# A second layer's modulation vectors: six products with ones and transposes, or 96 multiply-and-sums along the free axis

## The chip, the cores and the metric

The kernel runs on one core of one Trainium2 chip. The metric is the device time of one execution in microseconds. Engines are named as in the profile: PE (TensorE, with PEld for its weight loads), DVE (VectorE), ACT (ScalarE), POOL (GpSimd) and SP (SyncE, which issues nearly all DMAs here).

## The reference, cut to what matters

Two sequences, a prompt of 256 and a sample of 512 tokens of width 1024, go through a trunk of two layers. Layer 0 mixes with a bidirectional mLSTM, layer 1 with sliding-window attention; each then has a convolutional feed-forward block. In every layer six vectors of 1024 numbers, made from a condition vector, shift, scale and gate what flows through. All is float32.

```python
def trunk(x, c, adaln_w, adaln_b, norm_g, ...):
    for l in range(DEPTH):
        mod = jax.nn.silu(c) @ adaln_w[l] + adaln_b[l]
        sh1, sc1, g1, sh2, sc2, g2 = [t[:, None, :] for t in jnp.split(mod, 6, axis=-1)]
        h = rmsnorm(x, norm_g[l, 0]) * (1 + sc1) + sh1
        ...
        x = x + g1 * y
        h = rmsnorm(x, norm_g[l, 1]) * (1 + sc2) + sh2
        x = x + g2 * conv_ffn(h, ffn_w_up[l], ffn_conv_w[l], ffn_conv_b[l], ffn_w_down[l])
    return rmsnorm(x, final_g)

y_prompt = trunk(x_prompt, c_prompt, ...)
y_sample = trunk(x_sample, c_sample, ...)
```

`c` has one row of 1024 for the prompt and one for the sample, `adaln_w[l]` is 1024 x 6144. For one layer the modulation is thus a product of a 2 x 1024 matrix with a 1024 x 6144 matrix of 25 MB: little arithmetic and much to load.

## The kernel before, in words

Activations lie turned: the 1024 features are 8 blocks of 128 partitions, the 768 tokens of both sequences stand along the free axis. A modulation vector is wanted in the same form, so `mod[l]` is a tile of 128 x 48 x 2: feature block j of 48 (six vectors of eight blocks), and one column for the sample (0) and the prompt (1). Weights come as 512 KB tiles of 128 x 1024 through five buffers that share the name `raw`, fetched on SP's queue. A matrix product in full precision is made from two float32r halves: ACT casts the high half (`whi`, L275), DVE takes the difference (`wlo`, L276), and PE makes three products for one.

The modulation is made in three ways. `adaln` makes the first two vectors of layer 0 at the kernel's start on PE, while the weights stream in; the mLSTM's first product has to wait for it. `adaln_g` makes the other four of layer 0 on PE, in small pieces between the mLSTM's products. `adaln_v` makes all six of layer 1, mostly on DVE, and it is what the change touches. It is a Python generator, `self.fill`, which `mlstm` steps at fixed places of its code (after an evacuation of a product, as a rule); 49 steps use it up before the mLSTM ends. Its results are first needed in layer 1.

The old `adaln_v` goes through rows: for each of six groups (one vector of 1024 columns) and each of eight blocks k of 128 condition entries, a tile of `adaln_w` is fetched with the condition's entries on the partitions. DVE multiplies it by the condition's column `silc[:, k, s]`, one number for each partition, and adds it to the accumulator `acc` (tile `ada`), once for the sample and once for the prompt: L535 for k = 0, L537 for the others. After eight blocks the sum over the 128 partitions is left. PE makes it by four products of `acc` with a matrix of ones (the helper `mm`, L269, in the trace `ps<-ada,ones`), the result is copied to SBUF by DVE and ACT (L550, L551), turned by four transposes on PE (L554), and added to the bias into `mod` (L561). Two of the vectors also give `gain` (L565).

The order of instructions on the engines isn't that of the code throughout. The framework plans it with a simulated timeline: an instruction that comes later in the code can be listed earlier on its engine, where the plan has it ready. `manual_schedule` fixes the order by hand in places (the opening of the mLSTM among them, up to L1050), and `issue_after` puts an instruction behind a named one. Once planned, each engine's list is fixed, and SP's list of DMA issues with it: a wait at the head holds up everything behind it.

Lines that the prediction speaks of: L371 and L373 load constants, L399 loads x, L284 fetches every `raw` tile, L428 the rest of the first modulation's weights; L740 turns the mLSTM's gate rows into columns on PE; L839 and L840 multiply the mLSTM's scores with their decay on DVE, out of PSUM; L1190 is a multiply-and-reduce kind of instruction in layer 1's attention.

Of the kernel before, what the change touches and what calls it, by code (L numbers as in the profile page):

```python
# [11 lines left out]
F32 = mybir.dt.float32  # L12
R = mybir.dt.float32r
AF = mybir.ActivationFunctionType
ALU = mybir.AluOpType

P = 128
D = 1024
KC = D // P
# [31 lines left out]
AB = NG + 32  # L51
# [130 lines left out]
class Net:  # L182
# [185 lines left out]
    def setup(self):  # L368
        nc, io, cp = self.nc, self.io, self.cp
        self.cstt = cp.tile([P, NCST], F32, name="cstt")  # L370
        nc.sync.dma_start(self.cstt[:, :SOON], io["cst"][:, :SOON])  # L371
        self.kct = cp.tile([P, 3 * P], F32, name="kct")
        nc.sync.dma_start(self.kct[:, :P], io["kc"][:, :P])  # L373
        self.ident = self.kct[:, ID : ID + P]
        self.ones = cp.tile([P, P], F32, name="ones")
        nc.vector.memset(self.ones, 1.0)
        self.inv = cp.tile([P, 2], F32, name="inv")
        nc.vector.memset(self.inv, 1.0 / D)
        self.mhalf = cp.tile([P, 8], F32, name="mhalf")
        nc.vector.memset(self.mhalf, -0.5)  # L380
        self.silc = cp.tile([P, KC, 32], F32, name="silc")
        nc.vector.memset(self.silc, 0.0)
        nc.scalar.activation(
            self.silc[:, :, 0:2], self.cst(CT, 16).rearrange("p (k s) -> p k s", s=2), AF.Silu
        )
        self.mod = [cp.tile([P, 48, 2], F32, name=f"mod{l}") for l in range(DEPTH)]
        self.gain = [[cp.tile([P, KC, 2], F32, name=f"gain{l}{i}") for i in range(2)] for l in range(DEPTH)]


        self.zh = self.hp.tile([P, 4, 4, H], R, name="zh")  # L390
        self.zl = self.hp.tile([P, 4, 4, H], R, name="zl")
        flat = lambda z: z.rearrange("p a b c -> p (a b c)").rearrange("p (k t) -> p k t", k=KC)
        self.hh, self.hl = flat(self.zh), flat(self.zl)
# [121 lines left out]
    def adaln_v(self, l, pool):  # L515

        nc = self.nc
        stt = nc.vector.scalar_tensor_tensor
        rows = [(grp, k) for grp in range(6) for k in range(KC)]
        fetch = lambda grp, k: self.raw(  # L520
            self.io["adaln_w"][l, k * P : (k + 1) * P, grp * 1024 : (grp + 1) * 1024]
        )
        raw = fetch(*rows[0])
        yield
        for grp, k in rows:
            if k == 0:
                acc = pool.tile([P, 2, 1024], F32, tag="ada", name=self.nm("ada"), bufs=1)
            row = raw
            if (grp, k) != rows[-1]:
                raw = fetch(*rows[grp * KC + k + 1])  # L530
            for s in range(2):
                w = self.silc[:, k, s : s + 1]
                if k == 0:
                    with self.tc.issue_after(self.opened.ins):
                        nc.vector.tensor_scalar(acc[:, s], row, w, None, ALU.mult)  # L535
                else:
                    stt(acc[:, s], row, w, acc[:, s], ALU.mult, ALU.add)  # L537
            if k < KC - 1:
                yield
                continue  # L540

            with self.tc.high_priority():
                ps = self.ps()
                for s in range(2):
                    for b in range(2):
                        r0 = 32 * (2 * s + b)
                        self.mm(ps[r0 : r0 + 32, :], self.ones[:, :32], acc[:, s, b * 512 : (b + 1) * 512], True, True)
            sb = self.stg.tile([P, 2, 256], F32, tag="raw", name=self.nm("sb"), bufs=5)
            sb = [sb[:, z] for z in range(2)]
            nc.vector.tensor_copy(sb[0], ps[:, :256])  # L550
            nc.scalar.copy(sb[1], ps[:, 256:])  # L551
            pt = self.ps()
            for t in range(4):
                nc.tensor.transpose(  # L554
                    pt[:, t * P : (t + 1) * P], sb[t // 2][:, (t % 2) * P : (t % 2 + 1) * P], self.ident
                )
            src = pt.rearrange("p (t g s) -> p g t s", t=4, g=4)[:, :, :, 0]
            ab = self.cst(AB + 48 * l + 8 * grp, 8).rearrange("p (b t) -> p b t", b=2)
            dst = self.mod[l][:, grp * 8 : (grp + 1) * 8, :].rearrange("p (b t) s -> p b t s", b=2)
            for s in range(2):  # L560
                nc.vector.tensor_tensor(dst[:, :, :, s], src[:, 2 * s : 2 * s + 2], ab, ALU.add)  # L561
            i = {1: 0, 4: 1}.get(grp)
            if i is not None:
                for s in range(2):
                    stt(  # L565
                        self.gain[l][i][:, :, s], self.mod[l][:, grp * 8 : (grp + 1) * 8, s], 1.0,
                        self.cst(NG + (2 * l + i) * 8, 8), ALU.add, ALU.mult,
                    )
            yield
# [1200 lines left out]
def _colpack(a):  # L1770

    a = a.reshape(a.shape[:-1] + (-1, P))
    return np.moveaxis(a, -1, 0).reshape(P, -1)
# [29 lines left out]
def _shape_constants():  # L1803
    kc = np.zeros((P, NKC), np.float32)
    kc[:, ID : ID + P] = np.eye(P, dtype=np.float32)
    s = np.arange(P)[:, None]
    t = np.arange(P)[None, :]
    kc[:, MF : MF + P] = np.where(s > t, BIG, 0.0)
    kc[:, MB : MB + P] = np.where(s < t, BIG, 0.0)
    b = _buckets()  # L1810
    kc[b, OH + 510 - np.arange(511)] = 1.0
    rel = 255 - np.arange(511)
    kc[32, OH : OH + 511] = np.where(np.abs(rel) > WINDOW, -BIG, 0.0)
    return kc


def _pack(inp):
    arr = {}
    xs = np.concatenate([inp["x_prompt"][0], inp["x_sample"][0]], axis=0)
    arr["x"] = np.ascontiguousarray(xs.T.reshape(KC, P, T).transpose(1, 0, 2))  # L1820
    cst = np.zeros((P, NCST), np.float32)
    cst[:, NG : NG + 32] = _colpack(inp["norm_g"])
    cst[:, AB : AB + 96] = _colpack(inp["adaln_b"])
    cw = inp["ffn_conv_w"].reshape(DEPTH, 3, 44, P)
    cst[:, CW : CW + 264] = cw.transpose(3, 0, 2, 1).reshape(P, 264)
    cst[:, CB : CB + 88] = _colpack(inp["ffn_conv_b"])
    cst[:, HG : HG + 8] = _colpack(inp["mlstm_head_g"].reshape(1, D))
    cst[:, FG : FG + 8] = _colpack(inp["final_g"])
    cst[:, SK : SK + 16] = inp["attn_sink"][0][None, :]
    bg = inp["mlstm_b_gate"][0].reshape(2, 2, 4)  # L1830
    for d in range(2):
        for ty in range(2):
            cst[32 * d : 32 * d + 4, BG + ty] = bg[d, ty]
    c = np.stack([inp["c_sample"][0], inp["c_prompt"][0]], axis=1)
    cst[:, CT : CT + 16] = c.reshape(KC, P, 2).transpose(1, 0, 2).reshape(P, 16)
    arr["cst"] = cst
    arr["kc"] = _shape_constants()
    w = np.empty((N_UNITS, P, 2048), np.float32)
    wi = inp["mlstm_w_in"][0]
    for h in range(4):  # L1840
        for i in range(3):
            f = _unit_N if i == 2 else _unit_T
            w[U_MIN + 3 * h + i] = f(wi[:, i * D + h * 256 : i * D + (h + 1) * 256])
        w[U_MIN + 12 + h] = _unit_T(wi[:, 3 * D + h * 256 : 3 * D + (h + 1) * 256])
    wg = wi[:, 4 * D :].reshape(D, 2, 2, 4).transpose(0, 2, 1, 3).reshape(KC, P, 16)
    arr["wg"] = np.ascontiguousarray(wg.transpose(1, 0, 2).reshape(P, KC * 16))
    wa = inp["attn_w_in"][0]
    w[U_AIN] = _unit_T(wa[:, 1024:1280])
    w[U_AIN + 1] = _unit_N(wa[:, 1280:1536])
    for u in range(4):  # L1850
        cs = slice(u * 256, (u + 1) * 256)
        w[U_AIN + 2 + u] = _unit_T(wa[:, cs])
        w[U_MOUT + u] = _unit_T(inp["mlstm_w_out"][0][:, cs])
        w[U_AOUT + u] = _unit_T(inp["attn_w_out"][0][:, cs])
    for l in range(DEPTH):
        for p in range(NPART):
            u = U_FFN + (l * NPART + p) * 3
            w[u] = _unit_T(inp["ffn_w_up"][l][:, p * 256 : (p + 1) * 256])
            w[u + 1] = _unit_T(inp["ffn_w_up"][l][:, FF + p * 256 : FF + (p + 1) * 256])
            w[u + 2] = _unit_D(inp["ffn_w_down"][l][p * 256 : (p + 1) * 256])  # L1860
    arr["w"] = w
    arr["adaln_w"] = np.ascontiguousarray(inp["adaln_w"])
    arr["rel_bias"] = np.ascontiguousarray(inp["rel_bias"])
    return arr

# [24 lines left out]
```

## Time and profile before

| what | us |
|---|---|
| timed runs | 1814.29, 1816.16, 1816.62 |
| median | 1816.16 |
| profiled execution: span | 1814.6 |
| PE busy | 1782.7 (98%) |
| PEld busy | 1648.1 (91%) |
| DVE busy | 1374.9 (76%) |
| ACT busy | 887.4 (49%) |
| POOL busy | 487.8 (27%) |

The profile states the span of the profiled execution, from its first to its last instruction, and no time of its own beside it; the median is 1.6 us above that span. Rows of a timeline give start, duration, engine, line, operation, output and inputs, shape and count, and in brackets the idle time of the engine before it with what ended it. Matmuls overlap, so the distance between two starts tells more than a duration. Rows of one line's instructions give the shortest, median and longest duration in ns. The engines' queues are written with a q (SPq): they issue DMAs or wait.

### The profile page before, as it was taken

To read this page: it belongs to the slowest core of one execution; us is meant where nothing else is said; L and a number is where in the kernel's file an instruction comes from. 1 tells how busy PE (TensorE), PEld (TensorE's weight loads), DVE (VectorE), ACT (ScalarE), POOL (GpSimd) and SP (SyncE) were. 2 spreads that over 40 slices of the span, in tenths; PEclk is the share of its full clock that TensorE was granted. 3 is DMA by queue.
4 is the path that set the end of the run, shared out by engine and by line. 5 is a ranking of instruction groups with operands and counts; after the bars stand their busy time and mean duration, and the time that the engine had idled before them with its cause. 6 is when DMAs were issued, how large, how long until landed. Compare 5 with 4: busy or idle time off the path is not lost.

```text
span 1814.6 us, 28978 instructions
## 1 busy us (share of the span) xinstructions
PE 1782.7 (98%) x11278; PEld 1648.1 (91%) x11278; DVE 1374.9 (76%) x2141; ACT 887.4 (49%) x1794; POOL 487.8 (27%) x397
## 2 busy tenths in 40 slices
PE   7999999999999999999999999999999999999998
PEld 4988888889998999999999999889989999999998
DVE  4875777786799777777777867767998777777777
ACT  4553443444465444444444566765564444444443
POOL 3000000031024333333331313430144333333323
PEclk9999999999999999999999999999999999999999
DMA  9334565656212221222222321133122222222212
GB/s 340 113 119 146 167 208 189 200 167 221 86 58 72 69 70 62 69 68 70 70 71 83 116 86 50 53 95 129 56 83 70 70 71 70 70 70 70 70 36 70
DMA packets 64788, 184.01 MB, mean 101 GB/s; under 512 B 6199, under 2 KB 24759, under 8 KB 64652
## 3 DMA queue, kind: packets, MB, share of 16 engines
q1 hardware_dynamic: 64076, 181.65, 30.8%
q8 instruction: 88, 1.44, 0.3%
q10 hardware_dynamic: 576, 0.52, 0.1%
q14 instruction: 48, 0.39, 0.1%
HBM read 175.72 MB, written 6.43 MB: 100 GB/s over the span
## 4 chain that ended last, share of the span: by engine, by line
PE 83%; DVE 6%; DMA 4%; ACT 3%; issue 2%; POOL 1%; SPq 0%; POOLq 0%; DVEq 0%; ACTq 0%
PE ps L269 26%; PE pa L269 23%; PE ps L1370 10%; PE ps L1373 10%; PE ps L1371 10%; DMA raw<-in_w_dram 2%; DMA raw<-in_adaln_w_dram 1%; PE pa L1209 1%; DVE ada L537 1%; DVE wlo L276 1%; ACT whi L275 1%; DMA slab<-in_adaln_w_dram 1%; PE pa L1371 0%; PE pa L1370 0%; PE pa L1373 0%
## 5 line engine op out<-in xcount | busy, mean ns | idle before, releaser
L275 ACT CAST whi<-raw 128x1024 fp32r<-128x1024 f32 (+1 forms) x231 | 240.9, 1045 | 351.1 <-PE pa L269 145.3
L276 DVE TENSOR_TENSOR wlo<-raw,whi 128x1024 fp32r<-128x1024 f32 (+1 forms) x231 | 308.8, 1338 | 126.6 <-ACT whi L275 124.2
L269 PE MATMUL pa<-slab,whi 128*128 128x256 f32 (+1 forms) x1280 | 307.6, 335 | 0.0
L269 PEld LDWEIGHTS pa<-slab,whi 128*128 128x128 f32 x1280 | 222.2, 188 | 21.6 <-DVE slab L622 0.2
L622 DVE SCALAR_TENSOR_TENSOR slab<-pa,mod,slab 128x256 f32<-128x256 f32 (+1 forms) x320 | 187.1, 602 | 64.1 <-PE pa L269 63.9
L269 PE MATMUL pa<-slab,wlo 128*128 128x512 f32 (+1 forms) x640 | 205.7, 334 | 0.0
L269 PE MATMUL ps<-zh,whi 128*128 128x256 f32 (+1 forms) x560 | 187.9, 337 | 0.3 <-ACT zh L968 0.3
L269 PE MATMUL ps<-zl,whi 128*128 128x256 f32 (+1 forms) x560 | 184.1, 331 | 0.5 <-DVE zl L583 0.5
L269 PE MATMUL ps<-zh,wlo 128*128 128x256 f32 (+1 forms) x560 | 181.5, 330 | 0.0
L1370 PE MATMUL ps<-zh,whi 128*128 128x384 f32 x504 | 172.5, 342 | 4.3 <-ACT nt L1441 2.5
L269 PE MATMUL ps<-slab,whi 128*128 128x384 f32 (+2 forms) x704 | 172.0, 329 | 0.9 <-DVE slab L276 0.5
L1371 PE MATMUL ps<-zl,whi 128*128 128x384 f32 x504 | 169.9, 337 | 0.8 <-DVE zl L1327 0.8
L1373 PE MATMUL ps<-zh,wlo 128*128 128x384 f32 x504 | 169.2, 336 | 0.0
L1406 POOL TENSOR_TENSOR raw<-raw,raw 128x512 f32<-128x512 f32 x40 | 54.1, 1353 | 321.1 <-DVE wlo L276 247.1
L269 PEld LDWEIGHTS pa<-slab,wlo 128*128 128x128 f32 x640 | 120.4, 188 | 13.2 <-DVE wlo L276 0.4
L1622 POOL TENSOR_TENSOR slab<-slab 128x772 f32<-128x772 f32 x44 | 86.5, 1968 | 161.4 <-DVE slab L1610 149.5
L269 PEld LDWEIGHTS ps<-slab,whi 128*128 128x128 f32 x704 | 122.5, 188 | 3.4 <-ACT whi L275 0.9
L1609 DVE SCALAR_TENSOR_TENSOR slab<-slab,cstt,slab 128x771 f32<-128x771 f32 x88 | 104.2, 1186 | 26.4 <-ACT slab L1607 26.4
L537 DVE SCALAR_TENSOR_TENSOR ada<-raw,silc,ada 128x1024 f32<-128x1024 f32 x84 | 108.3, 1322 | 19.5 <-DMA raw<-in_adaln_w_dram 19.5
L269 PEld LDWEIGHTS ps<-zh,whi 128*128 128x128 f32 x560 | 106.4, 190 | 12.5 <-issue 3.5
L269 PEld LDWEIGHTS ps<-zl,whi 128*128 128x128 f32 x560 | 106.4, 190 | 12.4 <-issue 3.4
L269 PE MATMUL ps<-slab,wlo 128*128 128x384 f32 (+2 forms) x352 | 114.8, 328 | 0.1
(307 smaller groups left out, 4307.6 us busy)
## 6 DMA issues: line engine op xcount, KB each, us to landing
raw<-in_w_dram SPq DMA_DIRECT2D x208, 512.0 KB, 3.7
raw<-in_adaln_w_dram SPq DMA_DIRECT2D x84, 512.0 KB, 4.3
slab<-in_x_dram SPq DMA_DIRECT2D x12, 512.0 KB, 8.3
slab<-in_adaln_w_dram SPq DMA_DIRECT2D x11, 512.0 KB, 10.2
slab<-mrows SPq DMA_DIRECT2D x8, 384.0 KB, 4.7
xs<-slab SPq DMA_DIRECT2D x6, 512.0 KB, 3.8
bt<-brow SPq DMA_DIRECT2D x16, 192.0 KB, 3.2
slab<-xs SPq DMA_DIRECT2D x6, 512.0 KB, 7.3
```

Source lines behind the costliest of these rows:

```text
L269: self.nc.tensor.matmul(out, lhsT, rhs, start=start, stop=stop)
L275: nc.scalar.copy(hi, src)
L276: return nc.vector.tensor_tensor(lo, src, hi.bitcast(F32), ALU.subtract)
L537: stt(acc[:, s], row, w, acc[:, s], ALU.mult, ALU.add)
L622: return self.nc.vector.scalar_tensor_tensor(x, o, self.mod[l][:, gc + c, q : q + 1], x, ALU.mult, ALU.add)
L1209: nc.tensor.transpose(pp[:, ks], b.t[:, e, ks], self.ident)
L1370: mm(o, wh[:, k], hi[k], start=start and k == 0, stop=False, skip_group_check=True)
L1371: mm(o, wh[:, k], lo[k], start=False, stop=False, skip_group_check=True)
L1373: mm(o, wl[:, k], hi[k], start=False, stop=k == 3, skip_group_check=True)
L1406: tt(q[0], q[2], q[0], ALU.subtract)
L1609: stt(y[:, 1:], u[:, :-1], w(0), y[:, 1:], ALU.mult, ALU.add)
L1622: nc.gpsimd.tensor_tensor(y, y, yrow[:, j], ALU.mult)
```

## The change

The second layer's weights are turned on the host: `adaln_t[j]` is a tile with the 128 output features of block j on the partitions and the 1024 condition entries along the free axis. The condition, after its Silu, is written once to a scratch row in DRAM and read back broadcast to all 128 partitions as `row`, 128 x 2 x 1024. For each of 48 blocks and each of the two sequences DVE then makes one multiply-and-sum along the free axis, with the bias as the initial value, and writes a column of `mod`. The products with ones, the copies and the transposes are gone. The number of fetches (48 of 512 KB) and of steps (49) stays.

In `setup`, behind the Silu that makes `silc`:

```diff
+        crow = self.nt.tile([16, P], F32, tag="nt", name="crow0", bufs=8)
+        nc.sync.dma_start(crow, io["crow"])
+        nc.scalar.activation(crow, crow, AF.Silu)
+        rows = self.dp.tile([16, P], F32, name="crows")
+        nc.sync.dma_start(rows, crow)
+        self.crow = bass.AP(tensor=rows.tensor, offset=rows.offset, ap=[[0, 1], [1024, 2], [1, 1024]])
```

In `adaln_v`:

```diff
-        rows = [(grp, k) for grp in range(6) for k in range(KC)]
-        fetch = lambda grp, k: self.raw(
-            self.io["adaln_w"][l, k * P : (k + 1) * P, grp * 1024 : (grp + 1) * 1024]
-        )
-        raw = fetch(*rows[0])
+        row = pool.tile([P, 2, 1024], F32, name="crow")
+        nc.sync.dma_start(row, self.crow.to_broadcast([P, 2, 1024]))
+        junk = pool.tile([P, 1024], F32, name="junk")
+        mod = self.mod[l]
+        fetch = lambda j: self.raw(self.io["adaln_t"][j])
+        nxt = fetch(0)
         yield
-        for grp, k in rows:
...
-            with self.tc.high_priority():
-                ps = self.ps()
-                for s in range(2):
-                    for b in range(2):
-                        r0 = 32 * (2 * s + b)
-                        self.mm(ps[r0 : r0 + 32, :], self.ones[:, :32], acc[:, s, b * 512 : (b + 1) * 512], True, True)
...
+        for j in range(48):
+            w, nxt = nxt, fetch(j + 1) if j < 47 else None
+            with ExitStack() as order:
+                if j == 0:
+                    order.enter_context(self.tc.issue_after(self.opened.ins))
                 for s in range(2):
...
+                    nc.vector.tensor_tensor_reduce(
+                        out=junk, in0=w, in1=row[:, s], scale=1.0, scalar=self.cst(AB + 48 * l + j),
+                        op0=ALU.mult, op1=ALU.add, accum_out=mod[:, j, s : s + 1],
+                    )
+            i = {15: 0, 39: 1}.get(j)
             if i is not None:
                 for s in range(2):
                     stt(
-                        self.gain[l][i][:, :, s], self.mod[l][:, grp * 8 : (grp + 1) * 8, s], 1.0,
+                        self.gain[l][i][:, :, s], mod[:, j - 7 : j + 1, s], 1.0,
                         self.cst(NG + (2 * l + i) * 8, 8), ALU.add, ALU.mult,
                     )
             yield
```

On the host:

```diff
-    arr["adaln_w"] = np.ascontiguousarray(inp["adaln_w"])
+    arr["adaln_w"] = np.ascontiguousarray(inp["adaln_w"][:1])
+    arr["adaln_t"] = np.ascontiguousarray(inp["adaln_w"][1].T).reshape(48, P, D)
+    arr["crow"] = np.ascontiguousarray(c.T.reshape(16, P))
```

More of the change, by code (lines that the diff above doesn't have):

```diff
@@ L518, in adaln_v @@
         stt = nc.vector.scalar_tensor_tensor
-        rows = [(grp, k) for grp in range(6) for k in range(KC)]
-        fetch = lambda grp, k: self.raw(
-            self.io["adaln_w"][l, k * P : (k + 1) * P, grp * 1024 : (grp + 1) * 1024]
-        )
-        raw = fetch(*rows[0])
-        yield
-        for grp, k in rows:
[L526 to L530, printed above, removed]
-            for s in range(2):
[L532 to L540, printed above, removed]
-            with self.tc.high_priority():
-                ps = self.ps()
-                for s in range(2):
-                    for b in range(2):
-                        r0 = 32 * (2 * s + b)
-                        self.mm(ps[r0 : r0 + 32, :], self.ones[:, :32], acc[:, s, b * 512 : (b + 1) * 512], True, True)
[L548 to L562, printed above, removed]
```

## The prediction

> **What bounds the kernel now.** First the page's span and the chain of work that ended last, then a table of busy time by stretches.
>
> ```profile
> span 1814.6 us, 28978 instructions
> ```
> ```profile
> PE 83%; DVE 6%; DMA 4%; ACT 3%; issue 2%; POOL 1%; SPq 0%; POOLq 0%; DVEq 0%; ACTq 0%
> ```
> ```profile
> 62.00:112.00 50.00, 50.00 (x332) 45.82 (x331) 43.64 (x59) 23.20 (x37) 0.10 (x1) 1.00 0.52 171
> 112.00:122.00 10.00, 8.00 (x43) 6.80 (x43) 9.88 (x24) 7.12 (x17) 0.00 (x0) 0.83 0.17 54
> 122.00:430.00 308.00, 307.13 (x2130) 261.93 (x2130) 219.74 (x398) 123.79 (x316) 29.95 (x24) 1.00 0.53 174
> 430.00:1815.00 1385.00, 1367.28 (x8419) 1296.04 (x8418) 1070.58 (x1591) 704.68 (x1360) 439.63 (x346) 1.00 0.24 76
> ```
>
> The columns are the stretch, its length, busy time of PE, PEld, DVE, ACT and POOL, granted clock, DMA share and GB/s. The old modulation code works from 62 to 430 us. From 122 to 430 PE is busy 307.13 of 308 us, while DVE has 88 us free and the DMA engines are half used: PE is the bound, so what PE is spared there shortens the kernel. From 62 to 122 PE is full, except for one hole behind DVE at 113 us:
>
> ```profile
> 113.28 0.28 PE L269 MATMUL ps<-zh,whi 128*128 128x256 f32 x1
> 115.29 0.53 PE L740 MATMUL pa<-kct,slab 36*128 36x36 f32 x6 [1.74 <-DVE E L840]
> ```
> ```profile
> 119.16 0.63 PE L269 MATMUL ps<-zl,whi 128*128 128x512 f32 x1
> 119.59 0.63 PE L269 MATMUL ps<-zh,wlo 128*128 128x512 f32 x1
> ```
> ```profile
> 109.30 2.48 DVE L537 SCALAR_TENSOR_TENSOR ada<-raw,silc,ada 128x1024 f32<-128x1024 f32 x2 [0.81 <-DMA raw<-in_adaln_w_dram]
> ```
>
> PE starts nothing from 113.28 to 115.29, 1.9 us more than that product's own 0.12; the transposes of L740 wait for a PSUM buffer that DVE's products at L840 free, and those come behind a pair of modulation operations that stood at the head of DVE until a DMA landed. A few us later 512-column products start 0.43 us apart.
>
> **What goes from PE.** Each of six groups has four products with ones (in eight passes) and four transposes. The instructions of tile `ada` first, then PE alone around the second group.
>
> ```profile
> L537 DVE SCALAR_TENSOR_TENSOR ada<-raw,silc,ada x84: 1260/1277/2324, 68.0 to 416.4; 128x1024 f32<-128x1024 f32 x84
> L269 PEld LDWEIGHTS ps<-ada,ones x48: 106/109/110, 153.8 to 420.8; 128*32 128x32 f32 x48
> L269 PE MATMUL ps<-ada,ones x48: 592/593/617, 153.8 to 421.2; 128*32 128x512 f32 x48
> L535 DVE TENSOR_SCALAR ada<-raw,silc x12: 740/746/750, 63.5 to 387.9; 128x1024 f32<-128x1024 f32 x12
> ```
> ```profile
> 219.18 0.39 PE L269 MATMUL ps<-zh,whi 128*128 128x512 f32 x1
> 219.50 1.06 PE L269 MATMUL ps<-ada,ones 128*32 128x512 f32 x8
> 220.49 0.50 PE L269 MATMUL ps<-zl,whi 128*128 128x512 f32 x1
> 220.83 0.39 PE L269 MATMUL ps<-zh,wlo 128*128 128x512 f32 x1
> 221.06 0.39 PE L269 MATMUL ps<-zh,whi 128*128 128x512 f32 x1
> ...
> 226.12 0.40 PE L269 MATMUL ps<-zh,wlo 128*128 128x512 f32 x1
> 226.35 0.60 PE L554 MATMUL ps<-kct,sb 128*128 128x128 f32 x4
> 226.71 0.36 PE L269 MATMUL ps<-zh,whi 128*128 128x256 f32 x1
> ```
>
> I count by starts, as matmuls overlap. Neighbours of 512 columns start 0.23 us apart (220.83, 221.06). Round the ones the starts are 1.31 apart (219.18, 220.49), so the ones cost 1.08 us; the transposes cost 0.59 - 0.23 = 0.36 (226.12, 226.71). Eight passes of 593 ns thus cost far less than their sum, since they use different column strips at once. Six groups: 6 x 1.44 = 8.6 us. In the first group the transposes go in two pairs between small products:
>
> ```profile
> 158.25 0.44 PE L554 MATMUL ps<-kct,sb 128*128 128x128 f32 x2
> 158.62 0.62 PE L269 MATMUL ps<-raw,silc 128*32 128x256 f32 x2
> ```
>
> A pair costs 0.37 there, with a change of tile shape ahead of it of about 0.3; that group's transposes cost some 1.2 us and not 0.36. That brings the total to **9.5 us**, all in the stretch in which PE is the bound. With them go six copies each on DVE and ACT, twelve small adds, two of four PSUM banks for a while, and a `raw` buffer that a group's copies hold; none is on the path, so I count them at nothing. Their cover is DVE's 88 us and ACT's 184 us of free time from 122 to 430.
>
> **What comes on DVE.** A multiply-and-sum of 128 x 1024 isn't in this kernel, but the same instruction kind runs at L1190, with 384 and 256 elements:
>
> ```profile
> 1080.13 0.60 DVE L1190 CUSTOM_DVE_ANT_0 t<-pa,bt,nsk 128x384 f32<-128x384 f32 x1
> 1080.65 0.08 DVE L1190 DVE_READ_ACCUMULATOR2_ANT st<- 128x1 f32 x1
> 1080.65 0.48 DVE L1190 CUSTOM_DVE_ANT_0 t<-pa,bt,nsk 128x256 f32<-128x256 f32 x1
> ```
> ```profile
> 63.50 1.41 DVE L535 TENSOR_SCALAR ada<-raw,silc 128x1024 f32<-128x1024 f32 x2
> 64.83 0.68 DVE L279 SCALAR_TENSOR_TENSOR slab<-ps,slab 128x512 fp32r<-128x512 f32 x1
> ```
>
> The next operation starts 0.52 us after the 384-element one, and the accumulator's read hides under it. 128 more elements take 0.12 us more; 640 more make 0.60, so 1.12 us, and 1.2 if I scale the whole duration (0.60 x 1024 / 384 = 1.6 is the upper end). The pair at 109.30 ends after 2.48 us with an own duration of 1.27 each, so the old operation starts every 1.21 us. I take 1.2 for the new one, the value nearest to this row of the same size: a swap one for one. Only the twelve first-row operations get dearer: L535 runs every 0.67 (63.50 to 64.83 for two), so 12 x 0.54 = 6.5 us more on DVE over the kernel, less some 3 for the copies and adds that go. From 122 to 430 that disappears in free time.
>
> From 62 to 112 it doesn't: DVE is busy 43.64 of 50 us there, and its chain ends in the hole at 113. Of the 14 modulation operations before 113 two are first-row ones, so that stretch grows by 2 x 0.54 = **1.1 us**, and I let the hole grow by as much. Bounds: 0 (the planner puts the pair elsewhere) and 14 x 0.4 + 1.1 = 6.7, at 1.6 us each.
>
> [...] Here 2 us without a start was enough: the products at 119.16 run at half speed, and the stretch's granted clock is 0.83. [...]
>
> **What comes on DMA.** Setup gets a small load, a Silu on ACT and a small store; later comes a broadcast of 1 MB.
>
> ```profile
> 1.18 0.42 SPq L373 DMA_DIRECT2D kct<-in_kc_dram  x1
> 1.65 0.43 SPq L399 DMA_DIRECT2D slab<-in_x_dram  x1
> ```
> ```profile
> 4.00:40.00 36.00, 28.58 (x188) 16.43 (x189) 13.58 (x37) 12.04 (x34) 8.69 (x12) 1.00 1.04 397
> 48.00:60.00 12.00, 11.71 (x93) 11.08 (x93) 8.44 (x20) 6.05 (x14) 2.19 (x3) 1.00 0.00 0
> ```
> ```profile
> 42.64 21.30 SPq L284 DMA_DIRECT2D raw<-in_adaln_w_dram  x2
> ```
>
> Until 40 us the DMA engines are full, 397 GB/s, and PE's real work starts when the first layer's modulation has arrived. An issue takes SP 0.47 us (1.18 to 1.65); put ahead of the loads of x, the new load moves the whole stream by that: **0.5 us**. The store waits for the Silu; behind it on SP stand the loads of x and of modulation weights, and behind the Silu on ACT the squares of the first norm. I take it that the planner lists the store after some of those loads, which then keep the engines fed while SP waits. Bounds 0 and 1.4 (two issues and half a us of a dry queue). The tiny transfers move 16 KB, nothing at that rate.
>
> The broadcast waits only for the store, not for a buffer, and stands ahead of the first modulation fetch, which SP issued at 42.64. At 397 GB/s 1 MB is 2.6 us. Issued between 33 and 43, it ends before 48; the engines move 0 GB/s from 48 to 60, and the first reader is at 63.50. So nothing. If it came later than 60, the first multiply-and-sum would wait at the head of DVE, with weight splits (L276) behind it. The column fetches are 512 KB each as before, 48 as before, in the same buffers: nothing.
>
> **Sum.** -9.5 + 1.1 + 0.5 = -7.9. On the profiled span that is 1806.7; the median of the runs, 1816.16, is 1.6 above that span, so I forecast **1808.3 us**. A difference of 0.2%, 3.6 us, is about what can be told from none.
>
> **Rivals.**
> 1. The hole at 113 closes, because the planner orders DVE otherwise there. The hole takes 1.9 us and the half clock about eight products of 0.2 more, 1.6 (0.43 against 0.23): 3.5 us back, and the 1.1 isn't paid: -9.5 - 3.5 + 0.5 = -12.5, 1803.7. For it: one pair's place made the hole. Against: DVE's stretch isn't lighter. 0.13.
> 2. The broadcast is issued in the full stream, ahead of the mLSTM's first weights: +2.6 at the start, 1810.9. For it: it needs no buffer. Against: SP follows the program's order there. 0.07.
> 3. The operation and its accumulator's read run end to end, 1.27 + 0.08 = 1.35, 0.15 more each: 14 x 0.15 = 2.1 on the path, 1810.4. Against: the read at 1080.65 starts together with the next operation. 0.05. [...]
> 4. PE's saving turns into waits: the feeders (splits on DVE, fetches through five `raw` buffers) or a hole longer by 4 to 6 us take it back, 1813 to 1817, no change to be told. For it: the stretch to 113 is a DVE chain. Against: from 122 on PE waits for almost nothing. 0.13.
> 5. Slower: the multiply-and-sum costs two cycles an element at 1024, near 2.3 us. The 14 in the DVE-bound stretch then cost 14 x 1.1 = 15.4 more, in all -7.9 + 15.4 = +7.5, 1823.7. It decides from 7.9 / 14 = 0.56 us more each, 1.77 us. Against: the slope at L1190, though for another pair of operations. Other replanning mishaps counted in: 0.10.
>
> The likeliest has 0.52, with its own range 1804 to 1812. Faster by over 0.2%: 0.52 + 0.13 + 0.07 + 0.05 = 0.77; within: 0.13; slower: 0.10. The range 1802.5 to 1816.2 reaches down to rival 1 with a free start and up through most of rival 4; it leaves out the slower case and the outer edges.
>
> **What would show it.** Right: no `ada` products or L554-like transposes, PE's busy time down by 8 to 10 us before 430; the new operation starting 1.2 us after its predecessor; the first products of the mLSTM less than 1 us later than before; a hole near 113 of about 3 us; the broadcast landing before 60. Wrong: operations of over 1.6 us, new PE waits between 122 and 430, a first operation that waits for the broadcast, or a start that is later by 2 us or more.

## The result, and the profile after

| what | before | after |
|---|---|---|
| median of the timed runs, us | 1815.41 (4 runs, 1814.29 to 1816.62) | 1808.37 (4 runs, 1805.52 to 1809.53) |
| profiled span, us | 1814.6 | 1806.4 |
| PE busy, us | 1782.7 | 1773.1 |
| DVE busy, us | 1374.9 | 1384.8 |
| first product of the mLSTM starts, us | 35.88 | 36.21 |
| second gate columns start (the hole's end), us | 115.29 | 117.86 |
| first product of the mLSTM's output projection, us | 430.42 | 422.20 |

The change is faster: the ratio is 0.9958, 95% interval 0.9944 to 0.9972, 7.0 us in the medians. The forecast was 1808.3. One later execution of an experiment (e5, below) lasted 3505 us and is left out everywhere; that version was run again.

In the changed kernel the multiply-and-sum is L538 (`junk<-raw,crow,cstt`), the broadcast L526, the condition's load, Silu and store L387, L388 and L390; L740 and L840 of before are L720 and L820.

The page's span and its chain of work that ended last:

```profile
span 1806.4 us, 28907 instructions
```
```profile
PE 87%; DVE 5%; DMA 3%; ACT 3%; issue 1%; POOL 1%; SPq 0%; DVEq 0%; ACTq 0%; POOLq 0%
```

PE is the bound more than before, 87% of the chain in place of 83%. Busy time by stretches, in the columns of the same table above:

```profile
62.00:112.00 50.00, 49.83 (x329) 45.37 (x328) 42.30 (x69) 23.73 (x37) 0.10 (x1) 1.00 0.52 171
112.00:122.00 10.00, 6.95 (x40) 6.25 (x39) 9.91 (x22) 5.91 (x13) 0.00 (x0) 0.78 0.18 56
122.00:430.00 308.00, 307.63 (x2115) 268.89 (x2114) 229.31 (x472) 126.28 (x319) 34.41 (x25) 1.00 0.56 182
```

From 122 us PE is as full as it was, so what it no longer does became time. From 112 to 122 it is emptier: busy 6.95 us where it was 8.00, at a clock of 0.78 where it was 0.83. The landmarks in the first table say the same: 0.33 us lost at the start, 2.57 by the end of the hole, and 8.22 gained at the output projection, which stays to the end (8.18).

The instructions of the new line by themselves (ns of one: shortest, median, longest), then two places of DVE's timeline:

```profile
L538 DVE CUSTOM_DVE_ANT_0 junk<-raw,crow,cstt x96: 1266/1278/2195, 63.8 to 407.0; 128x1024 f32<-128x1024 f32 x96
```
```profile
63.84 1.28 DVE L538 CUSTOM_DVE_ANT_0 junk<-raw,crow,cstt 128x1024 f32<-128x1024 f32 x1
65.04 0.08 DVE L538 DVE_READ_ACCUMULATOR2_ANT mod<- 128x1 f32 x1
65.04 1.28 DVE L279 SCALAR_TENSOR_TENSOR slab<-ps,slab 128x512 fp32r<-128x512 f32 x2
...
101.57 1.29 DVE L538 CUSTOM_DVE_ANT_0 junk<-raw,crow,cstt 128x1024 f32<-128x1024 f32 x1 [4.77 <-DMA raw<-in_adaln_t_dram]
...
107.22 1.13 DVE L810 SCALAR_TENSOR_TENSOR E<-slab,aT,kct 128x128 f32<-128x128 f32 x4
...
111.84 1.28 DVE L538 CUSTOM_DVE_ANT_0 junk<-raw,crow,cstt 128x1024 f32<-128x1024 f32 x1 [1.85 <-DMA raw<-in_adaln_t_dram]
113.06 0.08 DVE L538 DVE_READ_ACCUMULATOR2_ANT mod<- 128x1 f32 x1
113.06 1.55 DVE L276 TENSOR_TENSOR PT<-E,PT 128x640 fp32r<-128x640 f32 x2
114.53 1.28 DVE L538 CUSTOM_DVE_ANT_0 junk<-raw,crow,cstt 128x1024 f32<-128x1024 f32 x1
115.73 0.08 DVE L538 DVE_READ_ACCUMULATOR2_ANT mod<- 128x1 f32 x1
115.73 1.13 DVE L810 SCALAR_TENSOR_TENSOR E<-slab,aT,kct 128x128 f32<-128x128 f32 x4
```

The next operation starts 1.20 us after the new one (63.84, 65.04), and the accumulator's read starts together with it. The bracket at 111.84 is the thing to see. DVE stands 1.85 us for a column's fetch (0.81 before), then runs that column's first half, a split, and its second half, and only at 115.73 the decay matrices (L810) that lead to L820, which frees PSUM for PE's next columns. On PE's timeline:

```profile
114.53 0.28 PE L269 MATMUL ps<-zl,whi 128*128 128x256 f32 x1
117.86 0.82 PE L720 MATMUL pa<-kct,slab 36*128 36x36 f32 x6 [3.05 <-ACT slab L278]
```

PE starts nothing for 3.33 us, 3.21 beyond that product's own 0.12; before it was 1.90. The bracket names ACT, whose write came last by the profile; DVE's L820 ends at 117.71, 0.15 us ahead of the start. In the kernel before, the first four decay matrices and the next ones stand here:

```profile
105.72 1.13 DVE L830 SCALAR_TENSOR_TENSOR E<-slab,aT,kct 128x128 f32<-128x128 f32 x4
...
113.17 1.14 DVE L830 SCALAR_TENSOR_TENSOR E<-slab,aT,kct 128x128 f32<-128x128 f32 x4
```

### The profile page after: what moved, and what is told of

Read it like the earlier page. It is cut to its first block, busy times and chain, and to the rows that moved or that the text cites. A ratio compares the mean times of both kernels' runs of the same rounds, so it can differ in the third digit from the quotient of the medians.

```text
span 1806.4 us, 28907 instructions
## 1 busy us (share of the span) xinstructions
PE 1773.1 (98%) x11206; PEld 1644.4 (91%) x11206; DVE 1384.8 (77%) x2219; ACT 887.8 (49%) x1789; POOL 488.2 (27%) x397
## 4 chain that ended last, share of the span: by engine, by line
PE 87%; DVE 5%; DMA 3%; ACT 3%; issue 1%; POOL 1%; SPq 0%; DVEq 0%; ACTq 0%; POOLq 0%
PE ps L269 28%; PE pa L269 24%; PE ps L1350 11%; PE ps L1351 10%; PE ps L1353 10%; DMA raw<-in_adaln_t_dram 1%; PE pa L1189 1%; DVE junk L538 1%; DMA slab<-in_adaln_w_dram 1%; DVE wlo L276 1%; PE pa L1350 0%; PE pa L1351 0%; PE pa L1353 0%; ACT zh L1301 0%; DMA raw<-in_adaln_w_dram 0%
## 5 line engine op out<-in xcount | busy, mean ns | idle before, releaser
L275 ACT CAST whi<-raw 128x1024 fp32r<-128x1024 f32 (+1 forms) x231 | 241.0, 1045 | 339.0 <-PE pa L269 144.4
L276 DVE TENSOR_TENSOR wlo<-raw,whi 128x1024 fp32r<-128x1024 f32 (+1 forms) x231 | 312.6, 1354 | 119.1 <-ACT whi L275 116.8
L538 DVE CUSTOM_DVE_ANT_0 junk<-raw,crow,cstt 128x1024 f32<-128x1024 f32 x96 | 125.2, 1305 | 25.1 <-DMA raw<-in_adaln_t_dram 24.5
```

Source lines behind the costliest of these rows:

```text
L275: nc.scalar.copy(hi, src)
L276: return nc.vector.tensor_tensor(lo, src, hi.bitcast(F32), ALU.subtract)
L538: nc.vector.tensor_tensor_reduce(out=junk, in0=w, in1=row[:, s], scale=1.0, scalar=self.cst(AB + 48 * l + j), op0=ALU.mult, op1=ALU.add, a ...
```

## The experiments

All differences are against the kernel before in the same session (medians 1815.71, 1816.17 and 1816.74 in three sessions) or against 1808.37 for the changed kernel, whose own session had 1815.41 before; the sessions thus differ by up to 1.3 us. "Hole" is the time for which PE starts nothing ahead of the second gate columns, less the last product's own distance; "half clock" is the length of the stretches in which the profile's clock is 0.5, from the mLSTM's first product to its output projection.

### The PE part and the DVE part apart

**e1_before_without_pe_part**: the old rows and accumulators, without what PE did with them.

```diff
-            with self.tc.high_priority():
-                ps = self.ps()
...
-            src = pt.rearrange("p (t g s) -> p g t s", t=4, g=4)[:, :, :, 0]
+            ab = self.cst(AB + 48 * l + 8 * grp, 8)
...
-                nc.vector.tensor_tensor(dst[:, :, :, s], src[:, 2 * s : 2 * s + 2], ab, ALU.add)
+                nc.vector.tensor_tensor(self.mod[l][:, grp * 8 : (grp + 1) * 8, s], acc[:, s, :8], ab, ALU.add)
```

> The kernel before without the products with ones, the copies and the transposes; the modulation of layer 1 is written from eight unsummed columns of the accumulator, so the layer computes with other numbers. DVE's 96 accumulations, their first-row price and the start stay as before. Theory (PE is the bound after 122 us, and its part is worth 9.5 us): 9.5 us below the kernel before, about 1806, with the hole at 113 us still about 1.9 us. Rival (a good part of PE's saving turns into waits for DVE or for buffers): 5 us below or less, 1810 or more, with new PE waits between 122 and 430 us.

Measured: 1801.59 us (4 runs, 1800.53 to 1805.11), ratio 0.9929 [0.9914, 0.9944], 14.1 us less. In its profiled execution, the longest of the four, the hole is still there, 2.07 us, but this time no half clock follows it:

```profile
115.16 0.53 PE L723 MATMUL pa<-kct,slab 36*128 36x36 f32 x6 [1.91 <-DVE E L823]
```
```profile
112.00:122.00 10.00, 7.83 (x51) 6.84 (x50) 9.87 (x24) 7.13 (x17) 0.00 (x0) 1.00 0.17 54
```

**e3_after_with_pe_part**: the changed kernel, with the ones, copies and transposes put back after each eighth column, on data that nothing uses.

```diff
+            if j % 8 == 7:
+                with self.tc.high_priority():
+                    ps = self.ps()
+                    for s in range(2):
+                        for b in range(2):
+                            r0 = 32 * (2 * s + b)
+                            self.mm(ps[r0 : r0 + 32, :], self.ones[:, :32], row[:, s, b * 512 : (b + 1) * 512], True, True)
...
+                for s in range(2):
+                    nc.vector.tensor_tensor(junk[:, 8 * s : 8 * s + 8], pt[:, 8 * s : 8 * s + 8], mod[:, :8, s], ALU.add)
```

> The changed kernel with the old PE part added back in its old rhythm, once after each eight columns: four products with ones (on the broadcast row), two copies, four transposes, two small adds whose result is thrown away. Theory (the gain is PE time): 9.5 us above the changed kernel, about 1818, above the kernel before by 2 to 3 us, since the longer hole and the later start are still paid. Rival (the gain came from elsewhere, from freed buffers and PSUM banks or another order of instructions): the sum of PE's starts grows by 9 us, but the time by less than 5, under 1813.

Measured: 1818.08 us (10 runs, 1816.52 to 1819.68), ratio 1.0018 [1.0008, 1.0027]. Against the changed kernel that is 9.7 us more. The two kernels bracket the change from both sides: taken from the old kernel the PE part is worth 14.1 us, put into the new one 9.7. The rest of the change, with its later start and its longer hole, costs 2.4 with the PE part in both kernels (1818.08 less 1815.71) and 6.8 with it in neither (1808.37 less 1801.59). So the gain is all on PE, and the rest by itself is slower than what it replaces. Why 14.1 and 9.7 differ isn't settled. By the profiles, the hole and the clock behind it don't explain it: the changed kernel and e3 have almost the same hole (3.21 and 3.04 us) and the same half clock (6.83); the kernel before and e1's profiled execution have 3.41 us of half clock each, and their spans still differ by 11.3, although e1 there has one more wait, of 1.96 us at 236.

### The free time of DVE

**e4_double_one_sequence**: from the second group on, the sample's multiply-and-sum is done twice, 40 more operations or 48 us of DVE.

```diff
-                for s in range(2):
+                for s in (0, 0, 1) if j >= 8 else (0, 1):
```

> The changed kernel with the sample's multiply-and-sum made twice for columns 8 to 47: 40 more operations of 1.2 us on DVE, 48 us, all after 122 us, where DVE has 79 us free. Theory (there DVE time is free and PE the bound): within 2 us of the changed kernel, 1808 to 1810. Rival (DVE's queue feeds PE closely, so an operation at its head delays weight splits): a third or more of the 48 us shows, 1824 or more.

Measured: 1814.13 us (10 runs, 1812.51 to 1817.69), ratio 0.9997 [0.9987, 1.0006], 5.8 us more than the changed kernel. The prediction's view, that DVE's 88 us of free time from 122 to 430 hide such work, holds for some seven eighths of the 48 us. The stretch, then PE's waits from 62 to 430 (us in total, times, longest):

```profile
122.00:430.00 308.00, 300.26 (x2079) 262.20 (x2078) 268.81 (x541) 125.18 (x314) 31.63 (x25) 0.99 0.54 173
```
```profile
PE ps L269 <- ACT whi L275: 6.7, 3, 3.6
PE pa L720 <- ACT slab L278: 2.2, 1, 2.2
PE ps L269 <- DVE wlo L276: 0.6, 2, 0.3
```

DVE is busy 268.81 of 308 us, on average far from full, and still PE waits 6.7 us in three places for halves of weights (L275); there the weight pipeline runs late. Both theories missed: the free time is neither all there nor gone. The 5.8 us are rather too low a price: this kernel's hole near 113 is shorter than the changed kernel's (2.34 us, with 3.41 of half clock behind it). By an estimate that is worth 2 us or more: 0.87 of hole and 1.2 to 1.7 of slow running.

### The hole

**e2_two_pairs_behind_hole**: in the changed kernel, the first group's last three columns (six operations) are put behind the copy of the second gate columns in DVE's list.

```diff
+                if 5 <= j < 8:
+                    order.enter_context(self.tc.issue_after(self.columned.ins))
...
-            nc.vector.tensor_copy(dst, pt.rearrange("p (t g) -> p t g", g=G))
+            self.columned = nc.vector.tensor_copy(dst, pt.rearrange("p (t g) -> p t g", g=G))
```

> The changed kernel with the multiply-and-sums of columns 5 to 7 put behind the copy of the second gate columns (the DVE copy that follows PE's wait in the hole). Theory (the hole is made by multiply-and-sums that wait for their column's DMA at the head of DVE, 4.8 us at 101.6 and 1.9 us at 111.8): the hole shrinks from 3.2 us to under 1 us, the stretch at half clock from 6.8 us to 3.4 or none, together 3 to 6 us, 1802.5 to 1805.5. Rival (the chain of the scores on DVE is late by itself, and the multiply-and-sums only fill its gaps): the hole stays at 3 us, 1808. Second rival: the moved operations open another hole later, 1808 or more.

Measured: 1803.06 us (4 runs, 1802.88 to 1805.04), ratio 0.9936 [0.9922, 0.9951]. The hole is gone, and with it all half clock. The stretch, and DVE's gate work:

```profile
112.00:122.00 10.00, 10.00 (x74) 9.37 (x73) 9.62 (x27) 6.53 (x21) 0.00 (x0) 1.00 0.18 48
```
```profile
104.84 1.13 DVE L812 SCALAR_TENSOR_TENSOR E<-slab,aT,kct 128x128 f32<-128x128 f32 x4
...
109.21 1.13 DVE L812 SCALAR_TENSOR_TENSOR E<-slab,aT,kct 128x128 f32<-128x128 f32 x4
```

From the first four decay matrices to the next DVE needs 4.37 us; in the changed kernel it is 8.51 (107.22 to 115.73). The second gate columns start at 112.05 in place of 117.86.

**e7_one_pair_less_held**: the same hold for columns 6 and 7 alone (`6 <= j < 8`).

> The changed kernel with only columns 6 and 7 of the first group held behind the second gate columns; column 5 stays ahead of them. It tells which wait of DVE makes the hole: the 4.77 us wait for a fetch near 101.6 us, or the 1.85 us wait at 111.8 with the pairs around it. My theory (the late one): the hole is under 1 us, the clock 1.00, and the time 1803 to 1804. Rival (the early one, ahead of column 5): a hole of 2 us or more remains, with at least 3.4 us of half clock, and the time is about 1806.

Measured: 1806.30 us (4 runs, 1805.40 to 1807.93), ratio 0.9947 [0.9934, 0.9961]. The hole is down to 0.83 us and the half clock is gone, as the theory has it, although the early wait, ahead of column 5, is even longer:

```profile
102.07 1.28 DVE L540 CUSTOM_DVE_ANT_0 junk<-raw,crow,cstt 128x1024 f32<-128x1024 f32 x1 [5.29 <-DMA raw<-in_adaln_t_dram]
```
```profile
114.20 0.54 PE L722 MATMUL pa<-kct,slab 36*128 36x36 f32 x6 [0.67 <-DVE E L822]
...
146.52 0.44 PE L740 MATMUL pa<-kct,slab 128*128 128x128 f32 x2 [2.13 <-ACT slab L736]
```

So the late wait and the two operations round it make the hole. The time is the rival's, though: PE now waits 2.13 us at 146 and some short waits stand ahead of it. A part of what the hole gave was lost a little later, at a wait which neither theory named.

**e6_before_two_pairs_behind_hole**: the same in the kernel before, for rows 6 and 7 of the first group.

```diff
+                        if grp == 0 and k in (6, 7):
+                            order.enter_context(self.tc.issue_after(self.columned.ins))
```

> The kernel before with only one edit: the modulation operations of the first group's columns 6 and 7 are held on DVE until the second gate columns are copied. My theory: the hole at 113 and the half clock behind it come from the place of these operations alone and cost 1.9 + 1.6 = 3.5 us, so the time is 1812.2 and the stretch from 112 to 122 has a granted clock of 1.00 and PE busy for over 9.8 of 10 us. Rival (the hole belongs to the whole DVE stretch, whatever stands at its end): a hole of over 1 us stays and the time is within 1 us of 1815.7.

Measured: 1814.92 us (10 runs, 1813.81 to 1816.09), ratio 0.9992 [0.9983, 1.0001]; 1.25 us less in the medians, 2.4 in the profiled spans. The hole is down to a wait of 0.34 us and the clock is whole:

```profile
112.00:122.00 10.00, 9.67 (x63) 8.70 (x64) 9.95 (x26) 5.91 (x16) 0.00 (x0) 1.00 0.18 55
```

The place of these operations made the hole in the old kernel too, but it was worth less there than the 3.5 us of the prediction's first rival; by the interval it may have been worth nothing. Why the median moves less than the trace does isn't settled.

**e9_cheap_first_column**: the first column's two operations are made about half as dear, to test the prediction's reason for the longer hole.

```diff
+                    if j == 0:
+                        nc.vector.tensor_scalar(junk, w, self.cst(AB + 48 * l + j), None, ALU.mult)
+                        nc.vector.tensor_copy(mod[:, j, s : s + 1], junk[:, :1])
+                        continue
```

> The changed kernel, but the first column's two multiply-and-sums are replaced by two plain multiplies of 128x1024 and two one-element copies; the first column's modulation is thus left out. It gives DVE back about 2 x 0.5 = 1.0 us at 64 us, the 1.1 us that the prediction put the growth of the hole down to. Theory of the prediction (dearer first rows make the hole longer): the hole shrinks from 3.21 to about 2.2 us, half clock from 6.83 to 3.41 us, and the time is 1808.4 - 1.0 - 1.7 = 1805.7. Rival (the end of DVE's wait for a fetch sets the hole, and that comes when it comes): the wait of 1.85 us at 111.8 grows by what was saved, the hole stays at 3.0 us or more, and the time is within 1 us of 1808.4.

Measured: 1808.90 us (4 runs, 1808.03 to 1810.27), ratio 0.9959 [0.9944, 0.9975]: no change. The hole is 2.89 us, the half clock 6.83.

```profile
120.21 0.82 PE L724 MATMUL pa<-kct,slab 36*128 36x36 f32 x6 [2.73 <-DVE E L824]
```
```profile
101.19 1.29 DVE L542 CUSTOM_DVE_ANT_0 junk<-raw,crow,cstt 128x1024 f32<-128x1024 f32 x1 [4.52 <-DMA raw<-in_adaln_t_dram]
...
114.19 1.28 DVE L542 CUSTOM_DVE_ANT_0 junk<-raw,crow,cstt 128x1024 f32<-128x1024 f32 x1 [1.61 <-DMA raw<-in_adaln_t_dram]
```

A microsecond less work on DVE at 64 us buys nothing: DVE waits for a fetch at 101 and again before the hole. The rival is right on the time; its detail, a wait longer than 1.85 us, isn't: it is 1.61, and the planner's list is another one (the second wait comes 2.4 us later).

**e10_fetch_two_ahead**: the column fetches are issued two columns ahead.

```diff
-        nxt = fetch(0)
+        nxt, after = fetch(0), fetch(1)
...
-            w, nxt = nxt, fetch(j + 1) if j < 47 else None
+            w, nxt, after = nxt, after, fetch(j + 2) if j < 46 else None
```

> The changed kernel with the column fetches issued two columns ahead in place of one; nothing else is changed. Theory (the hole is DVE standing at its head for a fetch): the waits of 4.77 and 1.85 us for the column fetches shrink to under 1 us together, the hole at 114.5 closes to under 1 us without half clock, and the time is about 1803.5. Rival (three of five buffers held by columns starve the weight fetches): new waits of PE for the weight splits of 4 us or more in all, and the time is 1808 or more.

Measured: 1809.53 us (4 runs, 1808.04 to 1811.85), ratio 0.9964 [0.9950, 0.9978]; not told from the changed kernel. The rival's time came, but not its waits for weight splits.

```profile
101.50 1.28 DVE L538 CUSTOM_DVE_ANT_0 junk<-raw,crow,cstt 128x1024 f32<-128x1024 f32 x1 [4.47 <-DMA raw<-in_adaln_t_dram]
...
115.44 1.28 DVE L538 CUSTOM_DVE_ANT_0 junk<-raw,crow,cstt 128x1024 f32<-128x1024 f32 x1 [0.95 <-DMA raw<-in_adaln_t_dram]
```
```profile
118.21 0.53 PE L720 MATMUL pa<-kct,slab 36*128 36x36 f32 x6 [0.93 <-DVE E L820]
...
157.85 0.33 PE L738 MATMUL pa<-kct,slab 128*128 128x128 f32 x1 [2.43 <-ACT slab L734]
```

The second wait halves, the hole shrinks to 1.09 us and loses its half clock; the first wait stays, and a new one of 2.43 us on PE, with 3.41 us of half clock behind it, stands against the gain. Issuing earlier in the program brought only one of the two fetches forward. The sixth column's fetch, which ends the first wait, was issued at 93.00 here and at 92.77 in the changed kernel. The seventh's came forward by 10.3 us, to 96.72, and the second wait is now for the eighth column. In the changed kernel the fetch that ends the wait at 111.84, the seventh of the columns, was issued when the split at 105.75, which takes 1.22 us, had released its buffer:

```profile
107.00 0.33 SPq L284 DMA_DIRECT2D raw<-in_adaln_t_dram  x1
```

### The start

**e8_broadcast_in_full_start**: the broadcast of 1 MB is issued behind the second part of x, in the stream that bounds the start.

```diff
-        row = pool.tile([P, 2, 1024], F32, name="crow")
-        nc.sync.dma_start(row, self.crow.to_broadcast([P, 2, 1024]))
+        row = self.crow_row
```

> The changed kernel with the 1 MB broadcast of the condition rows issued early, behind the second part of x, while the DMA engines are full, in place of 34 us. It prices the prediction's second rival. My theory: 1 MB at 397 GB/s delays the first mLSTM product by 2.6 us, from 36.2 to 38.8, and the total goes to about 1811. Rival (the start has room, or the transfer only takes the place of a later one): the first product moves by less than 0.5 us and the total stays at 1808.4.

Measured: 1810.75 us (10 runs, 1807.91 to 1814.06), ratio 0.9974 [0.9965, 0.9983], 2.4 us more than the changed kernel. The first product of the mLSTM in the changed kernel and in this one:

```profile
36.21 0.39 PE L269 MATMUL ps<-zh,whi 128*128 128x256 f32 x1 [0.28 <-ACT zh L948]
```
```profile
39.85 0.39 PE L269 MATMUL ps<-zh,whi 128*128 128x256 f32 x1 [0.28 <-ACT zh L947]
```

That is 3.64 us later, 1 us over the 2.6 that 1 MB at 397 GB/s makes. The trace shows both parts. The last sums of the first modulation reach DVE 2.68 us later, at 36.12 in place of 33.44:

```profile
33.44 0.43 DVE L457 COPY nt<-ps 128x256 f32<-128x256 f32 x1 [0.64 <-PE ps L447]
```
```profile
36.12 0.42 DVE L457 COPY nt<-ps 128x256 f32<-128x256 f32 x1 [3.08 <-PE ps L447]
```

The rest is the order on ACT, which has a copy (L458) on this path. In the changed kernel it runs ahead of the cast of the first weights (33.95 and 34.22); here it stands behind that cast, which waits for its weights until 36.64, and PE waits 0.98 us for the copy:

```profile
36.64 1.04 ACT L908 CAST whi<-raw 128x1024 fp32r<-128x1024 f32 x1 [7.79 <-DMA raw<-in_w_dram]
37.59 0.36 ACT L458 COPY nt<-ps 128x256 f32<-128x256 f32 x1
```

The profiled execution, the shortest of the ten, gets it all back in a hole of 1.89 us without half clock. Whether the hole is also why the medians moved by less isn't shown.

**e5_held_pairs_and_load_after_x**: e2, and the small load, Silu and store moved behind the first loads of x.

> The kernel with the last three first-group column pairs held behind the second gate columns (1803.06 us), and in addition the small load, the Silu and the store of the condition rows put behind the loads of x, so that x goes first on SP again. My theory (the +0.33 us at the first mLSTM product is the one issue of SP ahead of x): the first product comes back from 36.2 to 35.9 us and the total falls by 0.3 us, to some 1802.7, the best of the versions. Rival (the later start has another cause, the broadcast or the store): the first product stays at 36.1 to 36.2 and the total at 1803. The broadcast still lands before 60 us by both.

Measured: 1803.68 us (median of 4 runs, 1802.48 to 1804.35), ratio 0.9931 [0.9918, 0.9945]. Its first product can't be read from the profile that was kept, so e2 and e5 were run again side by side:

> The version with the first group's last three column pairs held behind the second gate columns, beside the next one on the same chip: 1803.1 again, within 1 us.

> The same version with the condition rows' load, Silu and store behind the loads of x. My theory (one SP issue ahead of x made the start 0.33 us later): the first mLSTM product at 35.9 us in place of 36.1 to 36.2, the time 0.3 us below the run beside it, too little to be told from it. Rival: the first product stays at 36.1 or later.

Measured: e11 1803.22 us (5 runs, 1802.81 to 1804.18) and e12 1803.39 us (5 runs, 1802.35 to 1804.92), both 0.9929 [0.9917, 0.9942]. The first products of e11 and of e12:

```profile
36.12 0.39 PE L269 MATMUL ps<-zh,whi 128*128 128x256 f32 x1 [0.28 <-ACT zh L950]
```
```profile
35.61 0.39 PE L269 MATMUL ps<-zh,whi 128*128 128x256 f32 x1 [0.29 <-ACT zh L944]
```

The start comes back by 0.51 us, about the 0.47 of one SP issue, but the total doesn't show it. That it is the issue of the small load alone isn't shown: the store moved too, from 4.54 to 33.40, and with it the broadcast, from 33.84 to 41.70. The version of e2 and e11 beats both kernels: 13.5 us less than before in its session, and its interval [0.9917, 0.9942] lies below that of the change [0.9944, 0.9972].

## Why the prediction was right

The sum was -9.5 + 1.1 + 0.5 = -7.9, and the profiled spans differ by 8.2. The mechanism is the one forecast, PE time saved where PE is the bound, less a longer hole and a later start. But two terms were too small, and their errors cancelled: that 1808.3 came within 0.1 us of the 1808.37 measured is luck, and the median before, 1816.16 when the forecast was made, was 1815.41 in the end.

**PE's part: -9.5 forecast, about -11 found.** From the first mLSTM product to the output projection the change took 8.55 us off (8.22 + 0.33). The hole grew by 1.31. By the distances between starts, against 0.23 and 0.12 us at full clock, the products behind it lost 1.6 us to the half clock before and 2.8 after, another 1.2. So all else took off about 8.55 + 2.5 = 11. From each removed instruction's start to the next start, the ones took 6.00 us and the transposes 2.75, 8.75 in all. Counted the prediction's way, with what the product ahead of a group loses, the six groups come to about 10.4: those at 281 and 338 us stand among products of another tile shape and cost 1.35 and 0.90 where the prediction had 1.08 and 0.36. What is left is not the removed instructions themselves: a pause at 217 (0.99 us between two starts) is gone, one at 294 (0.75) has come, and the rest is spread over neighbours. e3 gives the part back at 9.7 us, e1 at 14.1.

**The hole: +1.1 forecast, about +2.5 with its clock.** Here the step failed, not only its size. The prediction let the hole grow by the dearer first-row operations, 2 x 0.54. e9 takes about as much off, and the hole stays: DVE stands waiting for a fetch in between, and work ahead of that wait was free. What the traces show in its place is that DVE reaches the second decay matrices 2.56 us later (113.17 to 115.73) and PE comes to the hole 1.25 us later (113.28 to 114.53); the difference is the hole's 1.31. Of the 2.56, 1.50 are there at the first decay matrices already (105.72 to 107.22): they come behind a column that had kept DVE waiting until 101.57. Nearly all the rest, 1.04, is the wait behind them, 0.81 to 1.85 us. Its fetch is issued when a split returns its buffer, at 105.49 before and at 107.00 after, as much later as the decay matrices, so the issue alone would leave the wait as it was. But from issue to the end of the wait it took 4.84 us in place of 3.81. By the landing times, the fetch issued before it was under way until 110.56; in the old kernel the one before had landed at 105.57. That this made it longer is likely and not tested. The step also left the clock as it was; with the longer hole the half clock went from 3.41 to 6.83 us.

**The start: +0.5 forecast, +0.33 found**, and 0.51 between e11 and e12. One pair of profiles can't settle it: the first product stands at 35.43 to 35.88 in the three profiles with the old start and at 36.12 to 36.45 in the eight with the new one (e8 and e12 not counted), 0.55 apart in the mean. That is about the price of one SP issue ahead of x. The bound for the store's wait (1.4) wasn't reached: it was issued at 4.49, behind the first loads.

**What was to cost nothing.** The broadcast, issued at 33.97, landed 4.4 us later, far ahead of the first reader at 63.84. The new operation at 1.20 us is the value taken, so rivals 3 and 5 (1.35 and near 2.3 us) are out. That DVE's free time hides its dearer operations held for the 3 us or so at stake; e4 shows that it isn't all free, 5.8 us or more for 48.

**The rivals.** Rival 1, the hole closing through another order of DVE, didn't happen by itself, but e2 makes it happen: 1803.06 where the rival said 1803.7. Rival 2 was priced at 2.6 us: e8 shows 2.68 from the stream, 3.64 at the first product with ACT's other order, and 2.4 in the time. Rival 4 was near in one place only: the hole's growth took about 2.5 us back, not 4 to 6, and from 122 on PE waited almost nowhere.

**The clock.** "Here 2 us without a start was enough" was read from one hole and doesn't carry. Holes or waits of 1.90 (before), 1.96 (e1, at 236), 2.34 (e4) and 2.43 us (e10) had 3.41 us of half clock behind them, 2.89 (e9), 3.04 (e3) and 3.21 (after) had 6.83, but 1.89 (e8), 2.07 (e1) and 2.13 (e7) had none. So the lengths here are 3.41 us and twice that. The same step fits the lengths at full clock: in the kernel before it lasted from 11.68 to 117.49 us, 31 steps of 3.413, and from 120.91 to 1807.09, 494 of them; in the changed kernel from 11.85 to 117.67, 31, and from 124.49 to 1800.44, 491. With such steps laid over the profiles from the first full clock on, the holes sort, from the mLSTM's first product to its output projection, by how long PE ran nothing within one step:

| longest time without a running product in one step, us | half clock behind that step |
|---|---|
| 1.48 (before), 1.96 (e1, at 236), 2.18 (e4), 2.43 (e10), 2.75 (e4, at 417) | 3.41 us |
| 2.36 (e3), 2.67 (e9), 2.86 (after) | 6.83 us |
| 1.12 (e7), 1.25 (e8), 1.26 (e1, at 113), 1.38 (e4, at 267) | none |

So a hole near 2 us cost half clock when it brought some 1.5 us without a running product into one step, and none when the border of two steps cut it so that 1.38 or less fell into each. Two steps followed where the hole ran on past the end of its step, one where it ended before. Why, the runs don't show, and the sorting doesn't hold outside this stretch: e8 had 3.41 us of half clock from 27.09 on, behind steps with 1.30 and 0.62. In the kernel before, 1.48 us without a running product, less than half of a step, were enough for half rate.

## What to carry to other kernels

Find which engine is full where the change acts, and count removed matmuls by the distance between starts, not by their durations: eight passes of 593 ns were worth about 1 us. An operation that waits for a DMA at the head of an engine's list (1.85 us at 111.84 here, with the decay matrices listed behind it) belongs behind work that another engine is waiting for: moving six such operations back was worth 5.3 us more here, where the change itself brought 7.0. Work taken off such an engine ahead of a wait for data bought nothing here; first see what ends the wait.

## What the runs showed of the hardware beyond expectation

PE's half rate came in steps of 3.41 us (3.41 in the kernel before, 6.83 in the changed one, from the mLSTM's first product to its output projection), and whether a hole near 2 us brought one couldn't be told from its length: 1.90 (before) and 1.96 us (e1, at 236) did, 1.89 (e8), 2.07 (e1) and 2.13 (e7) didn't. It could be told, in the same stretch, from how long PE ran nothing within one step: 1.48 us (before) or more did, 1.38 (e4, at 267) or less didn't. A multiply-and-sum of 128x1024 in float32 costs 1.20 us from start to start (63.84 to 65.04), as much as a plain operation of that size (1.21, the pair at 109.30 in the kernel before), with the read of its accumulator hidden under the next operation (both start at 65.04). And 1 MB put into a full DMA stream delayed what waited for that stream by 2.68 us (e8), about the 2.6 that the stream's 397 GB/s make.
